# Row sums of a 16384 x 1024 matrix: the first load issued by GpSimd at the program's entry instead of SyncE

## The chip, the cores and the metric

The kernel runs on one core of one Trainium2 chip. A core has a vector engine (VectorE, DVE in the profile), a scalar engine (ScalarE, ACT), GpSimd (POOL), a tensor engine that this kernel doesn't use (PE), and SyncE (SP), which only issues transfers and waits. Each runs its own list of instructions, and they meet through semaphores. Data comes from the chip's memory (HBM) into the core's memory (SBUF, 128 partitions) through 16 DMA engines, which work through queues that SyncE, ScalarE and GpSimd fill. A name with a q behind it (SPq, POOLq) means the engine's sequencer: issuing, waiting, branching.

The metric is device time in microseconds (us). Before the change the median of 3 runs is 160.36 us (160.33 to 160.59).

## The reference

```python
def setup_inputs():
    batch, seq, dim = 32, 512, 1024
    return {"x": np.random.randn(batch, seq, dim).astype(np.float32)}

def reference(x):
    return np.sum(x, axis=-1).astype(np.float32)
```

The input has 16384 rows of 1024 float32 values, 67.1 MB; the output is one sum for each row, 64 KB.

## The kernel before

Each partition gets 128 rows. The rows are loaded in groups of 16 rows for each partition (128 x 16 x 1024 values, 8.39 MB), into three buffers of that size (`rows_0` to `rows_2`, line 77) which are used in turn. There are eight such groups. The last one is cut in two: its first 8 rows (`FIRST`, 4.19 MB) are loaded and summed first of all, and its other 8 rows last, in four small runs of uneven size (lines 167 to 186), so that little is left to sum once the last byte has landed.

The loads in their order are:

- `load_first`, 8 rows into `rows_0`, issued by SyncE (line 100);
- `load_0` to `load_6`, 16 rows each, issued by GpSimd (line 102). `load_0` goes to `rows_1`, `load_1` to `rows_2`, `load_2` to `rows_0`, and so on round the three. `load_0` and `load_1` wait for nothing; from `load_2` on GpSimd waits at line 156 until VectorE has summed the group that used the buffer before (semaphore `summed`);
- `run_0` to `run_3`, the last 8 rows in four pieces, issued by GpSimd as well once `summed` allows.

Every load has a semaphore of its own, which reaches 16 when all of it has landed. GpSimd's loads carry `single_packet=True`; SyncE's doesn't.

VectorE waits for each load and sums the group with one reduce (line 109, `vec`). For `load_6` and the last runs the rows are shared out between VectorE, which adds the two halves of a row and accumulates (line 118, `halves`), and ScalarE, which copies a row and accumulates (line 138, `act`). ScalarE stores the sums of the earlier groups (lines 215 and 216), and SyncE the last 16 columns (line 232) when VectorE and ScalarE are done.

The program begins with an entry block that the kernel's body doesn't write. In it GpSimd runs one bookkeeping instruction and four memsets of constants (line 248 in the profile), and all engines meet at a barrier, each after a drain of its own. Two more barriers follow (line 43), then a branch into the body. A transfer that the body issues therefore stands behind these barriers. `issue_first_load_at_entry` (line 9) runs when the program is finished: it finds the first DMA of SyncE in the body, which is `load_first`, asserts that it waits for nothing, takes it out and puts it into the entry block ahead of SyncE's drain. So SyncE issues `load_first` before the first barrier, and `load_0` is issued by GpSimd behind all three.

Of the kernel before, what the change touches and what calls it, by code (L numbers as in the profile page):

```python
# [8 lines left out]
def issue_first_load_at_entry(nc):  # L9

    main, *rest = nc.main_func.blocks
    SP = mybir.EngineType.SP
    for block in rest:
        insts = list(block.instructions)
        at = next(
            (k for k, i in enumerate(insts) if isinstance(i, mybir.InstDMACopy) and i.engine == SP),
            None,
        )
        if at is None:
            continue  # L20
        load = insts.pop(at)
        assert not load.sync_info.on_wait
        block.instructions = insts
        entry = list(main.instructions)
        k = next(k for k, i in enumerate(entry) if isinstance(i, mybir.InstDrain) and i.engine == SP)
        main.instructions = entry[:k] + [load] + entry[k:]
        return

# [2 lines left out]
def kernel(  # L31
# [4 lines left out]
):  # L36
    nc = tc.nc
    nc.at_finalize(issue_first_load_at_entry)


# [50 lines left out]
    def semaphore(name):  # L91
        return ctx.enter_context(nc.semaphore(name=name))
# [3 lines left out]

    def load(dst, src, k):
        sem = semaphore(f"load_{k}")
        if k == "first":
            nc.sync.dma_start(out=dst, in_=src).then_inc(sem, 16)  # L100
        else:
            nc.gpsimd.dma_start(out=dst, in_=src, single_packet=True).then_inc(sem, 16)  # L102
        return sem

    summed = semaphore("summed")
# [43 lines left out]
    t = bufs[0]  # L149
    block = block_of(t, 0, FIRST)  # L150
    landed = load(block, rows_from(tail, FIRST), "first")
    loads = [(landed, tail, block)]
    for g in range(last):
        t = bufs[(1 + g) % 3]
        if g > 1:
            nc.gpsimd.wait_ge(summed, g - 1)
        block = block_of(t, 0, BIG)
        loads.append((load(block, rows_from(g * BIG, BIG), g), g * BIG, block))
# [17 lines left out]
    for landed, first, block in loads[:-1]:  # L176
# [5 lines left out]
            (right6, 5 * dim + SIXTH), (right8, 7 * dim + EIGHTH))  # L182
    five, seventh, sixth, eighth = (
        load(dst, line[:, at : at + dst.shape[-1]], f"run_{k}")
        for k, (dst, at) in enumerate(runs)
    )
# [6 lines left out]
    landed, first, block = loads[-1]  # L193
# [70 lines left out]
```

## Time and profile before

| | |
|---|---|
| median of 3 runs | 160.36 us |
| the profiled execution's own time | 160.33 us |
| its span (first to last recorded instruction) | 159.0 us |
| VectorE busy | 121.6 us (76%) |
| ScalarE busy | 10.9 us (7%) |
| GpSimd busy | 6.1 us (4%) |
| SyncE's queue (q1), packets and MB | 288, 4.20 |
| GpSimd's queue (q0), packets and MB | 1424, 62.92 |
| mean rate of the transfers over the span | 422 GB/s |
| a reduce of 16 rows | 17.22 us |
| the reduce of `load_first` | 8.69 us, from 24.15 |
| `load_first`, issue to landing | 24.1 us |
| `load_0` to `load_6`, issue to landing | 40.4 us (median) |

Times count from the span's start, which here is SyncE's issue of `load_first`. Busy time of an engine leaves out its waits. The page cuts the span into 40 equal slices and gives each engine's busy share of a slice as a digit in tenths; the row DMA is the mean busy share of the 16 transfer engines. The chain of waits goes back from the last instruction through whatever released each step. The table of stretches gives, for each stretch of time, its length, the busy time and number of instructions of VectorE, ScalarE and GpSimd, the granted clock, the transfer engines' share and the GB/s; a packet counts wholly in the stretch in which it begins, so a short stretch can show a share over 1 and the one after it 0. The timeline lists start, duration, engine, line and operation, and in brackets how long the engine had been idle and what ended that. For a transfer it shows the issue alone, not the movement of the data.

### The profile page before, as it was taken

Reading aid. Unit: us, or ns where it says so; the run is one execution under the profiler, and the core shown is the slowest. Engines: PE = TensorE matmul, PEld = TensorE weight load, DVE = VectorE, ACT = ScalarE, POOL = GpSimd, SP = SyncE. Lnnn points to the kernel's source line nnn. Section 1 sums busy time; section 2 is a strip of 40 time slices with the busy share of each in tenths; the row PEclk is TensorE's granted clock in tenths of the full one; section 3 lists DMA queues with packets and bytes.
Section 4 is the critical chain, followed back from the end, with each engine's and each line's share of the span. In section 5 each row is a group of like instructions: output and inputs, shape, how many; then the busy total and the mean of one; then the engine's idle time right before and its main releaser. Section 6 shows DMA issues by size and latency. Waiting matters only on the chain.

```text
span 159.0 us, 124 instructions
## 1 busy us (share of the span) xinstructions
DVE 121.6 (76%) x43; ACT 10.9 (7%) x19; POOL 6.1 (4%) x15
## 2 busy tenths in 40 slices
DVE  0000009999998999949999599986999679995986
ACT  3000000000000000000000000000000000000995
POOL 3000000010001000010000100000000220000000
DMA  7999996997969969969969979799699699698994
GB/s 264 527 396 396 396 659 264 528 462 330 527 280 511 527 264 527 527 264 527 527 264 527 478 313 527 346 445 528 264 527 527 264 528 527 264 527 349 402 407 177
DMA packets 2000, 67.18 MB, mean 422 GB/s; under 512 B 624, under 2 KB 624, under 8 KB 848
## 3 DMA queue, kind: packets, MB, share of 16 engines
q0 software_dynamic: 1424, 62.92, 91.4%
q1 hardware_dynamic: 288, 4.20, 6.6%
q10 hardware_dynamic: 288, 0.06, 0.2%
HBM read 67.11 MB, written 0.07 MB: 422 GB/s over the span
## 4 chain that ended last, share of the span: by engine, by line
DMA 73%; DVE 24%; issue 1%; POOL 0%; POOLq 0%
DMA rows<-in_x_dram 73%; DVE sums L109 22%; DVE rows L118 2%; POOL rows L102 0%; DVE ends L118 0%; DVE sums L118 0%; POOLq L43 0%
## 5 line engine op out<-in xcount | busy, mean ns | idle before, releaser
L109 DVE TENSOR_REDUCE sums<-rows 128x16 f32<-128x16384 f32 (+1 forms) x7 | 111.9, 16000 | 31.8 <-DMA rows<-in_x_dram 31.8
L138 ACT ACTIVATE unread<-rows 128x1024 f32<-128x1024 f32 x9 | 9.1, 1014 | 145.1 <-DMA rows<-in_x_dram 145.1
L118 DVE CUSTOM_DVE_ANT_0 rows<-rows 128x512 f32<-128x512 f32 (+2 forms) x15 | 8.9, 663 | 2.6 <-DMA rows<-in_x_dram 2.6
L102 POOL DMA_DIRECT2D rows<-in_x_dram x9 | 4.9, 544 | 122.0 <-DVE sums L109 120.5
L138 ACT ACTIVATION_READ_ACCUMULATOR unread<-rows 128x1 f32 x9 | 1.7, 187 | 0.0
L138 ACT ACT_TABLE_LOAD x1 | 1.3, 1283 | 1.4 <-PEq L43 1.4
L118 DVE DVE_READ_ACCUMULATOR2_ANT sums<- 128x1 f32 x15 | 1.3, 84 | 0.0
L175 DVE MEMSET ends<- 128x1 f32 x2 | 0.1, 59 | 1.5 <-PEq L43 1.5
L102 POOL DMA_DIRECT2D ends<-in_x_dram x2 | 1.1, 541 | 0.0
L118 DVE CUSTOM_DVE_ANT_0 ends<-ends 128x257 f32<-128x257 f32 (+1 forms) x2 | 0.6, 360 | 0.0
L118 DVE DVE_READ_ACCUMULATOR2_ANT ends<- 128x1 f32 x2 | 0.2, 84 | 0.0
L248 POOL MEMSET const-float32-0.0<- 128x1 f32 x1 | 0.1, 98 | 0.2 <-issue 0.2
L248 POOL MEMSET const-bfloat16-1.0<- 128x1 bf16 x1 | 0.1, 101 | 0.0
L248 POOL MEMSET const-float32-1.0<- 128x1 f32 x1 | 0.1, 98 | 0.0
L248 POOL MEMSET const-uint8-127<- 128x1 uint8 x1 | 0.1, 98 | 0.0
## 6 DMA issues: line engine op xcount, KB each, us to landing
rows<-in_x_dram SPq DMA_DIRECT2D x1, 4096.0 KB, 24.1
rows<-in_x_dram POOLq DMA_DIRECT2D x1, 2816.0 KB, 27.8
rows<-in_x_dram POOLq DMA_DIRECT2D x1, 896.0 KB, 29.5
ends<-in_x_dram POOLq DMA_DIRECT2D x1, 256.0 KB, 29.6
ends<-in_x_dram POOLq DMA_DIRECT2D x1, 128.0 KB, 29.3
rows<-in_x_dram POOLq DMA_DIRECT2D x7, 40.4
out_dram<-sums ACTq DMA_DIRECT2D x1, 48.0 KB, 1.6
out_dram<-sums ACTq DMA_DIRECT2D x1, 8.0 KB, 1.5
```

The source lines that it names most:

```text
L102: nc.gpsimd.dma_start(out=dst, in_=src, single_packet=True).then_inc(sem, 16)
L109: return nc.vector.tensor_reduce(out=sums[:, j : j + n], in_=block, axis=mybir.AxisListType.X, op=mybir.AluOpType.add,)
L118: return nc.vector.tensor_tensor_reduce(out=src[:, :n], in0=src[:, :n], in1=src[:, n:], scale=1.0, scalar=0.0, op0=mybir.AluOpType.add, op ...
L138: nc.scalar.activation(out=unread[n_acts % len(unread)][:, :], in_=src, func=mybir.ActivationFunctionType.Copy, accum_out=sums[:, j : j + ...
L175: nc.vector.memset(w[:, -1:], 0.0)
L248: nc = _bacc.Bacc("TRN2", target_bir_lowering=False, num_devices=1)
```

## The change

`load_first` is issued by GpSimd, as all other loads are and with the same `single_packet=True`. The function that moves it to the entry block now looks for the first DMA of GpSimd in the body, again `load_first`, and puts it ahead of the first memset of GpSimd's constants, behind its bookkeeping instruction.

```diff
 def issue_first_load_at_entry(nc):
     main, *rest = nc.main_func.blocks
-    SP = mybir.EngineType.SP
+    POOL = mybir.EngineType.Pool
     for block in rest:
         insts = list(block.instructions)
         at = next(
-            (k for k, i in enumerate(insts) if isinstance(i, mybir.InstDMACopy) and i.engine == SP),
+            (k for k, i in enumerate(insts) if isinstance(i, mybir.InstDMACopy) and i.engine == POOL),
             None,
         )
...
         entry = list(main.instructions)
-        k = next(k for k, i in enumerate(entry) if isinstance(i, mybir.InstDrain) and i.engine == SP)
+        k = next(k for k, i in enumerate(entry) if isinstance(i, mybir.InstMemset) and i.engine == POOL)
         main.instructions = entry[:k] + [load] + entry[k:]
         return
...
     def load(dst, src, k):
         sem = semaphore(f"load_{k}")
-        if k == "first":
-            nc.sync.dma_start(out=dst, in_=src).then_inc(sem, 16)
-        else:
-            nc.gpsimd.dma_start(out=dst, in_=src, single_packet=True).then_inc(sem, 16)
+        nc.gpsimd.dma_start(out=dst, in_=src, single_packet=True).then_inc(sem, 16)
         return sem
```

In the order of the instructions GpSimd's list begins, after the change, with the bookkeeping instruction, `load_first`, the four memsets and the branch into the body, and then `load_0` and the rest as before. SyncE's list loses its first DMA and starts with its drain. The other engines' lists are the same.

## The prediction

> **What bounds the kernel now.** I began with the busy shares by slice and the chain of waits.
>
> ```profile
> DVE  0000009999998999949999599986999679995986
> DMA  7999996997969969969969979799699699698994
> ...
> DMA 73%; DVE 24%; issue 1%; POOL 0%; POOLq 0%
> ```
>
> The transfer engines are busy from the first slice to the last, while VectorE does nothing for six slices and still catches up. The 24% of VectorE on the chain are reduces that free a buffer for a transfer which then only queues. The next view is the table of stretches, which counts a packet where it begins.
>
> ```profile
> 0.00:24.15 24.15, 0.09 (x3) 1.28 (x1) 1.40 (x6) 1.00 1.03 434
> 24.15:50.70 26.55, 25.81 (x2) 0.00 (x0) 0.97 (x2) 1.00 1.00 434
> 50.70:70.00 19.30, 17.22 (x1) 0.00 (x0) 0.61 (x2) 1.00 1.00 435
> ```
>
> The last two columns are the transfer engines' share and GB/s. The rate is 434 to 435 GB/s at a share of 1.00. The 67.11 MB of the page at 434 GB/s need 154.6 us, so of the 159.0 us span only 4.4 lie outside an unbroken stream: a lead-in ahead of it and a tail of the last sums and the store behind it. The change touches only the lead-in. Here it is in fine stretches, followed by the issues of SyncE and GpSimd.
>
> ```profile
> 0.00:0.99 0.99, 0.00 (x0) 0.00 (x0) 0.20 (x4) 1.00 0.00 0
> 0.99:1.90 0.91, 0.09 (x2) 0.47 (x1) 0.00 (x0) 1.00 1.99 576
> 1.90:2.90 1.00, 0.00 (x0) 0.81 (x1) 0.96 (x2) 1.00 0.00 0
> 2.90:3.30 0.40, 0.00 (x0) 0.00 (x0) 0.23 (x1) 1.00 3.06 1311
> 3.30:4.20 0.90, 0.00 (x0) 0.00 (x0) 0.00 (x0) 1.00 0.00 0
> 4.20:4.50 0.30, 0.00 (x0) 0.00 (x0) 0.00 (x0) 1.00 4.05 1748
> ```
>
> ```profile
> 0.00 0.37 SPq L100 DMA_DIRECT2D rows<-in_x_dram  x1
> 0.24 0.10 POOL L248 MEMSET const-float32-0.0<- 128x1 f32 x1 [0.24 <-issue]
> ...
> 1.94 1.20 POOL L102 DMA_DIRECT2D rows<-in_x_dram  x2 [1.50 <-POOLq L43]
> ```
>
> SyncE issues at 0.00 and is done at 0.37; no packet begins before 0.99. Sixteen begin in 0.99 to 1.90 (576 GB/s times 0.91 us are 0.52 MB: one 32 KB packet for each of 16 engines), sixteen more in 2.90 to 3.30, and the next in 4.20 to 4.50, 1.21 us later. So full speed counts as begun at about 2.99 - 1.21 = 1.8 us. From there the stream is rigid: the time after is the time before plus whatever the lead-in grows.
>
> **The change part by part.** The sum stands on the profiled execution: 160.33 us for a span of 159.0, 0.03 under the median of 160.36.
>
> *SyncE's issue goes.* It ran 0.37 us in a place where nothing else waited to be streamed. Its going brings SyncE to the entry barriers sooner, worth nothing, because GpSimd will now be the last one there.
>
> *GpSimd's issue comes in.* It takes the first constant's place, so it starts no earlier than 0.24. After the barriers GpSimd's first DMA started late: the chain shows the gap.
>
> ```profile
> 1.32 0.61 issue
> 1.94 0.66 POOL rows L102
> 2.60 48.09 DMA rows<-in_x_dram
> ```
>
> GpSimd had passed its last barrier at 1.32 and waited for nothing the profile names, yet its first DMA began 0.61 later. GpSimd's first recorded work at the entry comes at 0.24, so the lower bound is 0.24. If the same 0.61 is paid by the first DMA wherever it stands, and GpSimd is ready for it near 0.14 (0.24 less the 0.1 of a constant's slot), it starts at 0.75, the upper bound. I take 0.75, since that row is the same operation in the same role: the first one that this engine issues. The issue then costs 0.53 us in the five that stand alone after a wait, and 0.66 the first time; I take 0.66, so it ends at 1.41.
>
> *From the issue's end to the first packet.* No row shows this for a GpSimd DMA on idle engines; this is the unknown cost. The nearest rows are SyncE's two. The first load: 0.99 - 0.37 = 0.62. Its closing store: issued at 157.59 for 0.35, no packets of its queue up to 158.40, so at least 0.46. Engines might start before GpSimd is done with an issue, so the bottom is nothing after the end, or even 0.3 ahead of it. The top is the trace's only look at GpSimd's queue near the start: issued at 1.94, and its first packets are in this answer for 6.6 to 7.0, none earlier.
>
> ```profile
> q0 software_dynamic: 16, 1.05, 604.9%
> ```
>
> That is at most 4.7 us from issue to packet, with the other queue's packets ahead of it. Between 0.9 (0.24 + 0.66 + 0) and 5.5 (0.75 + 4.7) I take SyncE's rows, 0.5: an ordinary issue on idle engines is nearer to them than to one that had to share. First packet at 1.41 + 0.5 = 1.91, against 0.99: 0.92 us later.
>
> On this gap the Trainium skill has a price, in DMA: Bandwidth & Descriptors, Specifications: first byte after about 1 us for a DMA that GpSimd's software prepares, about 0.6 us for SyncE's. As an estimate from that page the lead-in would grow by 0.4 plus GpSimd's later start of 0.24 to 0.75, giving 160.97 to 161.48 us; no run here shows the 1 us yet, and SyncE's 0.62 agrees with its half.
>
> *The ramp.* The first packets took until about 3.0 where later ones need 1.21: 0.8 us between a first packet at 0.99 and the effective start at 1.8. I keep it the same for GpSimd's packets. Bounds: 0 and 0.8 (they could run at full speed at once).
>
> *The load itself.* It loses the second queue. Before, its packets alternated with those of load 0 and it landed at 24.1; now it stands alone ahead of load 0 and lands near 1.9 + 0.8 + 9.7 = 12.4 (4.19 MB at 434 GB/s are 9.7). Load 0 and load 1 land in the same order and total, at 31.4 and 50.7 before, some 0.9 later now. The single-packet flag changes nothing I can price: 32 KB took 1.21 us on SyncE's queue, 64 KB 2.42 on GpSimd's (6.6 to 9.0 in the stretches), one rate.
>
> *What is moved behind it.* Four constants, GpSimd's drain, and the barrier at L248 wait for the issue. The engines passed it about 0.65 in the trace; now GpSimd needs 0.25 more after 1.41 (constants and drain ran from 0.24 to 0.49), and the release reaches the others at about 1.7, so all that follows is 1.05 later: ScalarE's table load (1.43 for 1.28 us, needed at 147.5), VectorE's two small memsets (needed at 154), and loads 0 and 1 on GpSimd, issued at about 3.0 and 3.7. They cost nothing: the first load keeps the engines occupied until 12.4. Without that cover each would cost the 1.05. Load 2's wait for the first reduce ends 11 us earlier (12.4 + 8.7 = 21.1 against 32.8), load 3's at about 49.5 (32.3 + 17.2), with load 2 in transfer until about 71. Nothing gains from that, because the stream had no hole to close.
>
> **Sum:** 160.33 + 0.92 = 161.25 us.
>
> **The rivals.**
>
> *No change.* The sixteen first packets began anywhere in 0.99 to 1.90 and yet the next set began together in 2.90 to 3.30. If something common held the first data until 1.8, a packet that begins at 1.9 loses about 0.1 and the ramp hides the later issue: 160.4. For it: that row. Against it: with one start in the trace, the ramp may as well run from the first packet. A rule of the Trainium skill points the same way (DMA: Bandwidth & Descriptors, Rules for kernel authors): which engine issues only shifts the issue time, as all use the same 16 engines. The equal 1.21 and 2.42 agree with it.
>
> *Faster.* GpSimd starts at 0.24, its descriptors are read 0.3 before its issue ends (0.24 + 0.66 - 0.3 = 0.6), and the packets run at full speed after half the ramp: effective start 1.0 against 1.8, 159.5; with a first packet at 1.4 and no ramp, 159.9. It decides in favour of the change once first packet plus ramp falls below 1.8. For it: the ramp may belong to SyncE's queue, whose first packets began spread over 0.91 us. Against it: the 0.61 and the 0.66, both measured.
>
> *Much slower.* A GpSimd issue needs 3.5 to 4.7 us before its packets run. For it: SyncE's queue got four rounds of packets (0.99, 2.9, 4.2, 5.4) before GpSimd's turn at 6.6, though from there on the two alternate; had it been ready at 5.4 it might have gone then (5.4 - 1.94 = 3.5). Against it: rounds may be lined up ahead. First packet at 0.24 + 3.5 = 3.7 to 0.75 + 4.7 = 5.45, so 2.7 to 4.5 later: 163.0 to 164.8, 163.9 in the middle.
>
> **How the numbers follow.** The forecast (161.25; with its two starts and ramps 160.65 to 162.3) has 0.62; much slower 0.15; no change 0.11; faster 0.12. The predicted time is 161.25. The range runs from 160.1, which takes in no change and the edge of faster, to 163.2, the near end of much slower; that leaves out about 0.10 below and 0.10 above. What a measurement here can tell is 0.2%, 0.32 us. Faster by more: 0.11, nearly all of its case. Within: 0.12, no change and the remaining 0.01. Slower: 0.62 + 0.15 = 0.77.
>
> **What would show it.** In the profile of the changed kernel: GpSimd's first DMA at 0.5 to 0.8, ahead of its constants; the stretches empty of packets until about 1.9, where 0.99 stood; full rounds 1.21 us apart from about 3.9; the first load landing near 12.4; loads 0 and 1 issued near 3.0 with no hole when the first ends; the last landing about 0.9 us later and the tail unchanged. First packets before 1.1 or a second round by 3.0 would make it wrong to the fast side, first packets after 3 to the slow side. A hole near 12, a slower rate than 434 GB/s with one queue, or a longer tail would say that I had the wrong place.

## The result and the profile after

The changed kernel takes 165.09 us (median of 5 runs, 164.97 to 165.18) against 160.36 before: a ratio of 1.0292 (95% interval 1.0277 to 1.0307), 4.73 us slower. The prediction said 161.25, with a range up to 163.2. The sign was right; the size and the range were not.

The busy shares of the changed kernel by slice (4.1 us each) show where the time is:

```profile
span 164.3 us, 124 instructions
...
DVE  0005960009999499986999599994999959996886
...
DMA  5987697999899599799989959979997995996994
...
DMA 67%; DVE 21%; POOL 1%; issue 1%; POOLq 0%
```

The transfer engines show 7 and 6 in the fourth and fifth slice, between 12 and 20 us, where before they showed 9 and 9. A single low digit also comes about because a packet counts in the slice in which it begins, but no later pair is as low before the last slices. The table of stretches (length; busy time and instructions of VectorE, ScalarE and GpSimd; clock; share of the transfer engines; GB/s) puts an edge on it:

```profile
0.00:2.10 2.10, 0.00 (x0) 0.00 (x0) 0.89 (x5) 1.00 0.00 0
2.10:2.60 0.50, 0.00 (x0) 0.00 (x0) 0.00 (x0) 1.00 3.90 1049
2.60:3.90 1.30, 0.00 (x0) 0.00 (x0) 0.00 (x0) 1.00 0.00 0
3.90:4.60 0.70, 0.00 (x0) 0.00 (x0) 0.00 (x0) 1.00 1.73 749
...
11.40:11.80 0.40, 0.00 (x0) 0.00 (x0) 0.00 (x0) 1.00 1.90 819
11.80:15.90 4.10, 1.56 (x3) 1.28 (x1) 1.06 (x2) 1.00 0.00 0
15.90:16.70 0.80, 0.80 (x1) 0.00 (x0) 0.00 (x0) 1.00 3.86 1311
```

The first packets begin from 2.1 on, and the second round is there by 3.9 to 4.6. The last round of the first load begins by 11.8 and takes 1.21 us. Then no data packet begins until 15.9, although loads 0 and 1 were meant to be queued since about 3. They weren't, as the timeline shows:

```profile
0.75 0.67 POOL L99 DMA_DIRECT2D rows<-in_x_dram  x1 [0.75 <-issue]
1.41 0.12 POOL L245 MEMSET const-float32-0.0<- 128x1 f32 x1
...
14.27 1.28 ACT L135 ACT_TABLE_LOAD   x1 [14.27 <-PEq L43]
...
14.37 8.69 DVE L106 TENSOR_REDUCE sums<-rows 128x8 f32<-128x8192 f32 x1
...
14.70 1.06 POOL L99 DMA_DIRECT2D rows<-in_x_dram  x2 [13.06 <-POOLq L43]
```

Loads 0 and 1 are issued at 14.70, where they stood at 1.94 before. All engines were held: ScalarE's table load went from 1.43 to 14.27. What held them is in the view of the entry block's line, which lists sequencer instructions too (shortest, median and longest duration in ns, first and last start in us). First the changed kernel, then the one before:

```profile
L245 SPq DRAIN  x1: 7/7/7, 0.0 to 0.0; - x1
...
L245 POOLq DRAIN  x1: 12544/12544/12544, 0.8 to 0.8; - x1
```

```profile
L248 POOLq DRAIN  x1: 184/184/184, 0.3 to 0.3; - x1
...
L248 SPq DRAIN  x1: 127/127/127, 0.4 to 0.4; - x1
```

GpSimd's drain took 184 ns before and 12,544 ns now, from 0.82 to 13.37. The first load, issued at 0.75, landed at 13.29, as the list of transfers has it (KB, us from issue to landing):

```profile
rows<-in_x_dram POOLq DMA_DIRECT2D x1, 4096.0 KB, 12.5
```

Before, SyncE drained in 127 ns, from 0.42 on, with the same load issued at 0.00 and not landed until 24.1.

### The profile page after: what moved, and what is told of

Its sections match the earlier page's. It is cut to its first block, busy times and chain, and to the rows that moved or that the text cites. A ratio compares the mean times of both kernels' runs of the same rounds, so it can differ in the third digit from the quotient of the medians.

```text
span 164.3 us, 124 instructions
## 1 busy us (share of the span) xinstructions
DVE 121.6 (74%) x43; ACT 11.0 (7%) x19; POOL 6.7 (4%) x16
## 4 chain that ended last, share of the span: by engine, by line
DMA 67%; DVE 21%; POOL 1%; issue 1%; POOLq 0%
DMA rows<-in_x_dram 49%; DVE sums L106 21%; DMA ends<-in_x_dram 18%; POOL rows L99 1%; DVE ends L115 0%; DVE sums L115 0%; POOLq L43 0%
## 5 line engine op out<-in xcount | busy, mean ns | idle before, releaser
L99 POOL DMA_DIRECT2D rows<-in_x_dram x10 | 5.4, 545 | 126.9 <-DVE sums L106 113.1
## 6 DMA issues: line engine op xcount, KB each, us to landing
rows<-in_x_dram POOLq DMA_DIRECT2D x1, 4096.0 KB, 12.5
```

## The experiments

Two theories stood against each other: that GpSimd's drain waits for GpSimd's own transfers and holds the barrier (drain theory), or that GpSimd can't follow up its first transfer on idle engines whatever the drains do, or only after some fixed delay. A third, the clock theory, came from a remainder. The profiled execution's own time exceeds the span by 1.30 us before and 0.80 after, and the 0.5 is how much later GpSimd's first recorded work begins (0.24 and 0.75).

Each ratio below is against the kernel before as measured beside that run: its median was 160.62 us (160.26 to 160.94) beside the load in the body, the kernel without drains, the load between the drains and the two loads, and 160.34 us (160.25 to 160.61) beside the other four.

**The load issued in the body, behind all three barriers.**

```diff
-    nc.at_finalize(issue_first_load_at_entry)
```

> GpSimd issues the first load as the first transfer of the body, behind all three entry barriers; nothing of GpSimd's is in flight when it drains. Drain theory (GpSimd's drain ends only when its own transfers have landed, and the barrier behind it holds loads 0 and 1 back): no hole behind the first load. The first issue moves to about 1.9, its first packet 1.37 later as in the changed kernel (0.75 to 2.12), so the stream counts as begun at about 4.0 in place of 1.8: 160.35 + 2.2 = 162.5 us. Queue theory (GpSimd's descriptor work can't take up the next transfers until its first one has landed, whatever drains do): the hole of 4 us stays, 166.5 us.

Measured: 162.67 us, ratio 1.0122 (1.0098 to 1.0145). Issues of GpSimd and its entry drain:

```profile
1.90 1.72 POOL L98 DMA_DIRECT2D rows<-in_x_dram  x3 [1.46 <-POOLq L42]
```

```profile
L244 POOLq DRAIN  x1: 184/184/184, 0.3 to 0.3; - x1
```

The drain is back at 184 ns, three loads are issued in a row and the packets begin at 3.27, 1.37 after the issue, without a gap later. The queue theory's 166.5 is out. Issued later, the load costs 2.05 us by the measured time (162.67 against 160.62) and 2.5 us by the profiled spans (161.54 against 159.03), about half of what it costs at the entry.

**The changed kernel without GpSimd's drains.** The three drains ahead of the body are left out; the load stays ahead of the constants.

```diff
+        drains = [
+            i for i in insts[:at] if isinstance(i, mybir.InstDrain) and i.engine == POOL
+        ]
-        block.instructions = insts
+        block.instructions = [i for i in insts if i not in drains]
...
+        entry = entry[:k] + [load] + entry[k:]
+        main.instructions = [
+            i for i in entry if not (isinstance(i, mybir.InstDrain) and i.engine == POOL)
+        ]
```

> The changed kernel without GpSimd's three drain instructions ahead of the body. Drain theory: loads 0 and 1 are issued at about 2.7, no hole; what is left is the later lead-in (1.0 us), less the 0.5 that the clock of the measurement seems to start later (first recorded work of GpSimd at 0.75 in place of 0.24): 160.8 to 161.1 us. Queue theory: no change against the changed kernel, 165.1 us.

Measured: 160.98 us, ratio 1.0025 (1.0014 to 1.0036).

```profile
0.74 0.67 POOL L106 DMA_DIRECT2D rows<-in_x_dram  x1 [0.74 <-issue]
...
2.14 1.05 POOL L106 DMA_DIRECT2D rows<-in_x_dram  x2 [0.51 <-issue]
```

```profile
11.80:12.40 0.60, 0.00 (x0) 0.00 (x0) 0.00 (x0) 1.00 0.25 109
12.40:13.20 0.80, 0.00 (x0) 0.00 (x0) 0.00 (x0) 1.00 2.84 1229
```

Load 0's packets begin at 12.4, as those of the first load end. The three drains are the whole hole: the span falls from 164.30 to 160.12.

**The load between the first drain and the second.**

```diff
-        k = next(k for k, i in enumerate(entry) if isinstance(i, mybir.InstMemset) and i.engine == POOL)
+        drains = [k for k, i in enumerate(entry) if isinstance(i, mybir.InstDrain) and i.engine == POOL]
+        k = drains[0] + 1
```

> The first load stands behind the constants and the first drain, ahead of the two barriers whose drains come next. Drain theory: the second drain now waits for the landing in place of the first, about 12 us long; the hole is one barrier round (0.3 us) shorter, the clock starts at 0.24 with the constants: 165.2 to 165.6 us. Rival (only the first drain, or the constants queued behind the load, make it wait): no hole, 161.2 to 161.6 us.

Measured: 165.71 us, ratio 1.0319 (1.0295 to 1.0343), 0.1 above the expected interval. The next barriers' line (here L44) holds the wait now:

```profile
L246 POOLq DRAIN  x1: 184/184/184, 0.3 to 0.3; - x1
```

```profile
L44 POOLq DRAIN  x2: 41/6508/12976, 1.2 to 14.4; - x2
```

The first drain is short, the second takes 12,976 ns, the third 41. The pause between the last packet of the first load and the next one is 0.3 us shorter, as expected (packets begin at 12.56 and 16.44, in the changed kernel at 11.78 and 15.94). The profiled execution was the slowest of the four, 166.15 us, and its first load took 13.04 us from issue to landing in place of 12.55. So what waits isn't one particular drain, and the constants don't matter: it is whichever drain of GpSimd's comes next while its transfer is in flight.

**The load behind the constants, ahead of the drain.**

```diff
-        k = next(k for k, i in enumerate(entry) if isinstance(i, mybir.InstMemset) and i.engine == POOL)
+        drains = [k for k, i in enumerate(entry) if isinstance(i, mybir.InstDrain) and i.engine == POOL]
+        k = drains[0]
```

> The changed kernel with the load behind the four constants and still ahead of the drain. Drain theory: same drain, same hole, landings within 0.2 us of the changed kernel's on the trace's clock. Clock theory (the measured time starts with the first recorded work of a computing engine): it starts at 0.24 in place of 0.75, so 165.6 us; without it 165.1 to 165.3 us.

Measured: 165.75 us, ratio 1.0339 (1.0325 to 1.0353). The span is 164.31, that of the changed kernel to 0.01, with a drain of 12,535 ns. Being ahead of the constants is worth nothing on the trace's clock; the measured 0.66 more agrees with the clock theory's 0.5 rather than with no difference, and the two profiled executions, with equal spans, differ by just 0.51 (165.61 and 165.10).

**Two and three loads at the entry.**

```diff
-        load = insts.pop(at)
-        assert not load.sync_info.on_wait
+        loads = [insts.pop(at) for _ in range(2)]
+        assert not any(i.sync_info.on_wait for i in loads)
...
-        main.instructions = entry[:k] + [load] + entry[k:]
+        main.instructions = entry[:k] + loads + entry[k:]
```

> GpSimd issues the first load and load 0 at the entry, both ahead of the constants. Drain theory: the drain lasts until load 0 has landed too, to about 32; the hole stands there in place of 13 and is as long (about 4 us to full speed): 165.1 us, 0.3 either way. Rival (a delay of fixed length or place after the entry: code, barrier, descriptor work, over by about 15 us): load 0 covers it, 160.8 to 161.2 us.

> GpSimd issues the first load, load 0 and load 1 at the entry. Drain theory: the drain lasts until load 1 has landed, near 51.6; VectorE, held at the same barrier, starts its first reduce (8.7 us) only then, and load 2 waits for that: hole of about 12 us to full speed in place of 4, 173 to 175 us. Rival (delay of fixed length after the entry): no hole, 161 us.

Measured: 165.20 us with two, ratio 1.0283 (1.0263 to 1.0304); 176.08 with three (the same edit with `range(3)`), ratio 1.0979 (1.0962 to 1.0996). The drain of the one and then of the other, and a stretch of the one with two:

```profile
L245 POOLq DRAIN  x1: 31324/31324/31324, 1.3 to 1.3; - x1
```

```profile
30.20:35.10 4.90, 1.53 (x3) 1.28 (x1) 0.53 (x1) 1.00 0.00 0
```

```profile
L245 POOLq DRAIN  x1: 50365/50365/50365, 1.7 to 1.7; - x1
```

The drain goes along with the last landing: it ends at 32.60 and 52.09 where load 0 and load 1 landed at 32.48 and 51.92. With two loads the hole moved to 32 and cost the same, so a delay of fixed place is out. With three the hole is 51.6 to 63.3 as expected, but the total is 1 us over the expected interval: The last load landed at 171.2, and what the expectation left out is VectorE's backlog. It reduced without a break from 53 on, started on load 6 only at 164.45, though that had landed at 161.5, and finished 2.7 us after the last byte; in the changed kernel it takes 0.4.

**SyncE as cover.** GpSimd keeps the first load at the entry, and SyncE issues loads 0 and 1 there. The function that moves a load is now called three times, with the issuing engine and the kind of instruction that the load is put ahead of.

```diff
 def issue_first_load_at_entry(nc):
+    issue_at_entry(nc, mybir.EngineType.Pool, mybir.InstMemset)
+    issue_at_entry(nc, mybir.EngineType.SP, mybir.InstDrain)
+    issue_at_entry(nc, mybir.EngineType.SP, mybir.InstDrain)
...
-        nc.gpsimd.dma_start(out=dst, in_=src, single_packet=True).then_inc(sem, 16)
+        if k in (0, 1):
+            nc.sync.dma_start(out=dst, in_=src).then_inc(sem, 16)
+        else:
+            nc.gpsimd.dma_start(out=dst, in_=src, single_packet=True).then_inc(sem, 16)
```

> GpSimd keeps the first load at the entry, ahead of the constants; SyncE issues loads 0 and 1 at the entry, at 0.0 and 0.4. Drain theory: GpSimd's drain is as long as ever (first load shares the engines with load 0 packet by packet, so it lands near 31), but load 1 on SyncE's queue still streams to about 51, so no hole; the stream starts with SyncE's packet at 1.0 as before the change. On the trace's own clock the end is that of before; by the measured time, if its clock starts with GpSimd's first recorded work (0.75 in place of 0.24), 0.5 less: 159.8 to 160.0 us. Rival (a long drain costs by itself, wherever the cover): 163 to 165 us.

Measured: 159.98 us, ratio 0.9977 (0.9969 to 0.9986). The first load from issue to landing, then the drains:

```profile
rows<-in_x_dram POOLq DMA_DIRECT2D x1, 4096.0 KB, 33.3
```

```profile
L253 POOLq DRAIN  x1: 33313/33313/33313, 0.8 to 0.8; - x1
...
L253 SPq DRAIN  x1: 125/125/125, 0.9 to 0.9; - x1
```

The drain is the longest but one of all, and the kernel isn't slower: SyncE's load 1 streams on until 55.8 while GpSimd waits until 34.1. The first load landed at 34.05, where about 31 was expected, and load 1 at 55.8 in place of 51, since load 2, issued at 44.11, shared the engines with it. A long drain by itself costs nothing here; an empty queue behind it does. SyncE's drain takes 125 ns with two of its transfers issued and not landed. This version beats both kernels by the measured time, but not on the trace's clock: its span is 159.26 against 159.03, so the 0.2% lie in where the measured time begins.

**The kernel before, without the constants that nothing reads.**

```diff
-        main.instructions = entry[:k] + [load] + entry[k:]
+        main.instructions = [
+            i for i in entry[:k] + [load] + entry[k:] if not isinstance(i, mybir.InstMemset)
+        ]
```

> The kernel before, without the four constants that GpSimd writes at the entry and that nothing in this kernel reads. Clock theory: all landings stay, and the measured time starts with ScalarE's table load at 1.4 in place of 0.24: 159.2 us. If the measured time starts with SyncE's issue or ahead of it: 160.3 to 160.4 us.

Measured: 159.09 us, ratio 0.9924 (0.9910 to 0.9937), with a span of 158.98 against 159.03: no part of the work became faster. Here the own time exceeds the span by 0.04 us, and the first recorded work of an engine other than the table load is VectorE's memset:

```profile
0.00 0.37 SPq L102 DMA_DIRECT2D rows<-in_x_dram  x1
1.43 1.28 ACT L140 ACT_TABLE_LOAD   x1 [1.43 <-PEq L45]
1.50 0.09 DVE L177 MEMSET ends<- 128x1 f32 x2 [1.50 <-PEq L45]
```

Start of that work plus what the own time has over the span is 0.24 + 1.30 before, 0.75 + 0.80 after, 1.50 + 0.04 here, and 1.53 to 1.55 in all the other runs. That the table load at 1.43 doesn't count, which the expectation had as the start, rests on this kernel alone: with it the sum would be 1.47.

## Why the prediction was wrong

The step that failed is the paragraph on what is moved behind the issue: "They cost nothing: the first load keeps the engines occupied until 12.4." It gave GpSimd 0.25 us after its issue for "constants and drain", their length in the trace of before, where GpSimd had nothing in flight. The trace showed a drain only in a state that the change ends. The account of GpSimd's list in the section on the change leaves the drains out too: they and the barriers stand between the four memsets and loads 0 and 1. With a transfer of its own out, the drain ends 0.08 to 0.17 us after the last of them has landed (six kernels, drains of 12.5 to 50.4 us); what it is in the drain that waits, no trace shows. So the cover that I named, the first load's streaming, was the very thing waited for: loads 0 and 1 couldn't be issued until it was over, and no length of cover on GpSimd's queue would have helped, as the entry with two loads shows. The prediction did name the sign: "A hole near 12" would say that it had the wrong place.

By its terms, in us:

| term | predicted | measured | from |
|---|---|---|---|
| lead-in | +0.92 | +1.09 | spans: 160.12 without the drains, 159.03 before |
| hole behind the first load | 0 | +4.18 | spans: 164.30 after, 160.12 without the drains |
| the measured time begins later | 0 | -0.51 | first recorded work at 0.75 and 0.24 |
| sum | +0.92 | +4.76 | own times of the profiled executions: 165.10 - 160.33 = 4.77 |

These are single profiled executions; spans of the kernel before lie between 158.9 and 159.6 us, so the first two terms are good to a few tenths.

*Bound and stream.* Right: the stream is rigid, and its rate with one queue is unchanged (64 KB in 2.42 us, 32 KB in 1.21).

*The lead-in.* Near in each part, with errors that partly cancel. The issue starts at 0.75 (predicted 0.75) and takes 0.67 (0.66); the exact start is partly luck, as GpSimd's bookkeeping instruction ended at 0.17, not 0.14, and the gap was 0.58, not 0.61. From the issue's end to the first packet are 0.70 (0.5): 2.12 - 1.42. The ramp is 0.65 (0.8): the second round starts at 3.97 on the first engine, 3.97 - 1.21 - 2.12. The 160.65 to 162.3 that the prediction gives for the forecast "with its two starts and ramps" isn't what they add up to: starts of 0.24 and 0.75 with a ramp of 0 or 0.8 give 159.9 to 161.25. From the issue's start to the first packet it took 1.37 in all seven kernels in which GpSimd's first load met idle engines. The page DMA: Bandwidth & Descriptors of the Trainium skill, section Specifications, has about 1 us to the first byte of such a DMA, without a starting point; the measurement decides.

*The hole's parts.* The data of the first load ends between 12.4 and 13.0 on the different engines, it is reported as landed at 13.29 (predicted 12.4), the drain ends at 13.37, the last barrier is passed at 14.16, GpSimd's issue starts 0.54 later, its packets 1.24 after that at 15.94, and the ramp is paid a second time, at about 0.6. From 12.4 to 15.94 that is 3.5, or 4.1 with the ramp.

*The rivals.* "Much slower" had nearly the size (163.9) and the wrong mechanism: it asked for 3.5 to 4.7 us from issue to packet, where 1.37 was measured. In the kernel before, loads 0 and 1 were ready near 1.94 + 1.37 = 3.3, if the 1.37 holds there too, and got their turn at 6.6, so SyncE's packets were lined up ahead, as the argument against that rival had it. "No change" by a common start fell as well: the ramp follows the first packet, wherever it is. "Faster" fell with the issue at 0.75. The range ended at the near edge of a rival with the wrong cause; none of my cases had the entry's barrier wait for the load.

*The clock.* That the measured time doesn't begin with SyncE's issue I had not seen. It worked for the change, by 0.51.

## What to carry to other kernels

Before moving an instruction across a barrier, ask of every drain or wait that it jumps ahead of whether its short duration holds only because nothing was in flight. Here the entry is a fair place for a transfer that SyncE issues and a bad one for GpSimd's, unless another queue carries the stream until the drain is over. And cover must come from work that isn't itself what the stalled engine waits for.

## What the runs showed of the hardware and the measurement that I had not expected

- GpSimd's drain waits until GpSimd's own transfers have landed (it ended 0.08 to 0.17 us later in six kernels), and for no others: 33.3 us with its load landing at 34.05, while SyncE's load 1 was in flight until 55.8. SyncE's drain takes 125 to 127 ns with SyncE's transfers issued and not landed.
- A GpSimd queue that joins a busy one doesn't get the next packet: ready near 3.3 by the 1.37 us of the other runs, it was served at 6.6, two of SyncE's rounds of packets having gone out between. With SyncE as cover it was ready near 2.1 (0.74 + 1.37) by the same reckoning and served at 6.5.
- The first DMA that GpSimd issues in the entry or behind a barrier starts late: 0.58 us after the bookkeeping instruction in the changed kernel, where the next one starts 0.54 after the last barrier, and 0.61 after it in the kernel before. Behind the four constants it was 0.41 after the last of them.
- The measured time behaves in all ten kernels as if it began with the first recorded work of a computing engine, leaving out SyncE's issue and, by 0.07 us in the one kernel that can tell, ScalarE's table load. Differences of some tenths of a microsecond at the entry are to be read from the landings on the trace's clock instead.
